# A four-layer mixer stack: decay sums broadcast by DMA, S5 inputs loaded from another queue, S5 output matrices in a ring of three

## The chip, the cores and the metric

The kernel runs on one core of one Trainium2 chip. The metric is the device time of one execution in microseconds: the median of three runs was 2107.67 (2106.01 to 2112.61). A single further execution was recorded by the hardware profiler and took 2112.38. All times inside the kernel are from that execution.

## What is computed

A sequence of 256 tokens of width 2048 passes through four layers, each a different mixer, and after each one the result is added to the residual and normalised:

```python
h = x
for i in range(4):                     # ssd, fox, mla, s5
    out = mixer[i](h, ...)
    h = layer_norm(ALPHA * h + out, ln_g[i], ln_b[i])
```

Layer 0 (ssd) works on 8 groups of 8 heads. For a group it needs, in each of two chunks of 128 tokens, the running sums `acs` of the decay of each head, and from them a 128x128 matrix per head:

```python
seg = acs[..., :, None] - acs[..., None, :]
decay = exp(where(l >= s, seg, -inf))
y_diag = einsum('bcgls,bcgels,bcsgep->bclgep', cb, decay, xdt)
...
yg = yg * rsqrt(mean(square(yg), -1) + RMS_EPS)     # per group, ahead of the output matrix
```

Layer 1 (fox) is attention with a forget gate over 16 heads. Layer 2 (mla) is attention with low-rank projections. Layer 3 (s5) is a diagonal state-space layer: an input map, a scan over time of complex states, and an output map, then a gated linear unit. Everything is 32-bit.

## The kernel before

**Projections.** Every large matrix product is done in three passes. `half` (L89) loads half of a weight block, 512 KB, into one of 7 `raw` buffers through the SyncE queue (SP). ScalarE (ACT) rounds it to `whi` (L100), VectorE (DVE) forms the remainder `wlo` (L101); there are 4 buffers of each. TensorE (PE) then multiplies hi by hi, hi by lo and lo by hi (`mm3`, L107 to L109). One half is 24 matmuls of 256 columns (`proj_T`) or 12 of 512 columns (`proj_tok`).

**Order.** The program is written as one stream of projections. After each half `C.tick()` (L56) advances a counter and runs what `C.defer(n, fn)` (L51) had put off by n ticks. That is how side work (decays, scores, scans, transposes) gets its place between the halves. A scheduler then fixes the order on each engine; every engine and every DMA queue works strictly in its own order, so a waiting instruction holds all behind it. That goes for SP too: its queue carries the weight loads of all layers in one line.

**Layer 0, `ssd` (L424).** `group(g)` (L513) makes z (8 halves into `pt`), then B, C and four x strips (12 halves into `cps`), each with a short convolution. `decay(g)` (L501) works on `arena[:, 0:2048]`, called `seg`: four small GpSimd (POOL) DMAs bring the sums of two heads each to one partition of `rows`, four `partition_broadcast` instructions (L506) spread them over 128 partitions, 16 DVE instructions (L510) subtract and mask, ACT takes one exponential of 2048 columns (L511). `scores` multiplies by the score matrix (L535). `within` (L565) uses `seg` as weights of the matmuls `yd`. `gate` (L560) multiplies by z on POOL (L562) and squares on ACT (L563), `across` (L582) adds the state part on POOL (L587), takes an inverse square root in small DVE steps (`rsqrt`, L192) and scales on ACT (L593). `turn_y` (L598), 4 ticks later, transposes the result on PE (`ypt`, L605). Of group g, `within`, `across` and `turn_y` run while group g+1 is at its z and B halves.

**Layer 1, `fox` (L623)** carries the parameters of layer 3 along: `s5_params` (L905) is a generator, stepped once per head, whose 16 steps on POOL make the input, output and kernel matrices of S5 (`wn`, `pn`, `kt`) and store them to DRAM (`W_d`, `P_d`, `K_d`). Each step needs a tile `bc` of 128 KB of inputs, of which there are 4 buffers, loaded by SP (`load_bc`, L1048). PE transposes and multiplies what a step made (`wp`, L1028, and `kp`, L1035) one step later.

**Layer 3, `s5` (L1112).** Four input strips (`u_strip`), then 16 `z_tile`s of two halves each; between them the strips are turned, mapped into states (`enter`, matmuls `vp`), scanned on DVE (`scan`, L1149, three pieces of 1, 2 and 1 strips, about 1.9 us of it per tick), and mapped out in 8 halves (`y_half`, L1299: matmuls `near` with a tile `shifts` from `K_d`, then `far` with a tile `mats` from `P_d`). The tiles `mats` and `shifts` share one ring of 2 buffers, loaded by POOL's DMA queue (L1137, L1146). `y_load` of a half asks for its `mats`, then its `shifts`, and is called when the half before has been written into the program.

Of the kernel before, what the change touches and what calls it, by code (L numbers as in the profile page):

```python
# [19 lines left out]
P = 128  # L20
T = 256
# [402 lines left out]
def ssd(C, hT, out):  # L424
    nc, A = C.nc, C.A
    mm, tr = nc.tensor.matmul, nc.tensor.transpose
    G, E, NH = 8, 8, 64
    with C.tc.tile_pool(name="ssd", bufs=1) as sp, C.tc.tile_pool(name="ssd_c", bufs=1) as vp, C.tc.tile_pool(name="ssd_t", bufs=1) as tp:
# [69 lines left out]

        seg = arena[:, 0:2048].rearrange("p (e c l) -> p e c l", e=E, c=2)

        def decay(g):  # L501
            rows = tp.tile([P, 512], F32, tag="rows", name="rows", bufs=1)
            for r in range(4):
                nc.gpsimd.dma_start(rows[32 * r:32 * r + 1], acsT[g * E + 2 * r:g * E + 2 * r + 2, :])
            for r in range(4):
                nc.gpsimd.partition_broadcast(arena[:, r * 512:(r + 1) * 512], rows[32 * r:32 * r + 1])  # L506
            for c in range(2):
                for e in range(E):
                    s = acs_t[c][:, g * E + e:g * E + e + 1]
                    nc.vector.scalar_tensor_tensor(seg[:, e, c], seg[:, e, c], s, upm, op0=ALU.subtract, op1=ALU.min)  # L510
            nc.scalar.activation(arena[:, 0:2048], arena[:, 0:2048], AF.Exp)  # L511

        def group(g):  # L513
            zs = arena[:, 2048 + (g % 2) * 1024:2048 + (g % 2 + 1) * 1024].rearrange("p (t f) -> p t f", t=2)
# [11 lines left out]
            def scores():  # L526
                cbp = C.aux("cbp")
                for c in range(2):
                    cs = slice(c * P, (c + 1) * P)
                    mm(cbp[:, cs], bT[:, cs], cT[:, cs], start=True, stop=True)  # L530
                tr(cbp[:, 256:384], bT[:, 0:P], C.ident)
                S["btok"] = vp.tile([P, P], F32, tag="btok", name="btok")
                nc.scalar.copy(S["btok"], cbp[:, 256:384])
                m8 = arena[:, 0:2048].rearrange("p (e x) -> p e x", e=E)
                nc.vector.tensor_tensor(m8, m8, cbp[:, None, 0:256].to_broadcast([P, E, 256]), op=ALU.mult)  # L535

            C.defer(2, scores)
            xp = []

            def turn_x(k, xc):  # L540
# [41 lines left out]
            def across():  # L582
                xs, off, sq = S["xs"], S["off"], S["sq"]
                ops = C.aux("ops")
                mm(ops, cT[:, P:], S["st"], start=True, stop=True)
                nc.vector.tensor_tensor(heads(off), heads(ops), bc(eacs, g), op=ALU.mult)
                nc.gpsimd.tensor_tensor(xs[1], xs[1], off, op=ALU.add)  # L587
                gate(1)
                ms = tp.tile([P, 2], F32, tag="ms", name="ms")
                nc.vector.tensor_scalar(ms, sq, 1.0 / 512, 4 * RMS_EPS, op0=ALU.mult, op1=ALU.add)  # L590
                rs = C.rsqrt(ms, 2, "gr")
                for c in range(2):
                    nc.scalar.activation(xs[c], xs[c], AF.Copy, scale=rs[:, c:c + 1])  # L593
                C.defer(4, turn_y)
                if g == G - 1:
                    C.load_res(A["x"])

# [18 lines left out]
        for g in range(G):  # L616
            group(g)
        return C.out_layer(0, lambda cb, **kw: C.proj_tok([A["ssd_o"][cb, q] for q in range(8)], yT, **kw),
                           [(tp, t, 1, 1) for t in ("xs0", "xs1", "xdt0", "xdt1", "xdd", "st", "rows", "gb")],
                           [[(C.hp, f"h{n}{c}", 1) for n in "hl"] for c in range(4)], out)  # L620


# [282 lines left out]
def s5_params(C, sp, sq):  # L905
# [142 lines left out]
    def load_bc(n):  # L1048
        if n < 16:
            bcs[n] = sq.tile([P, 4, 4, 16], F32, tag="bc", name="bc", bufs=4)  # L1050
            nc.sync.dma_start(bcs[n], A["s5_bc"][n])

    turns = None
    for n in range(2):
# [57 lines left out]
def s5(C, hT, out):  # L1112
# [8 lines left out]
    with C.tc.tile_pool(name="s5", bufs=1) as sp, C.tc.tile_pool(name="s5_w", bufs=1) as wp, C.tc.tile_pool(name="s5_t", bufs=1) as tp:  # L1121
# [11 lines left out]
        uX, U = {}, {}  # L1133

        def mats(src):
            t = wp.tile([P, 1024], F32, tag="mats", name="mats", bufs=2)
            nc.gpsimd.dma_start(t, src)  # L1137
            return t

        def shifts(ft, h2):  # L1140

            t = wp.tile([P, 848], F32, tag="mats", name="shifts", bufs=2)
            for e in range(2):
                src = C.K_d[ft, h2, e].rearrange("i g b f -> i (g b f)")
                src = bass.AP(src.tensor, src.offset, [[16, L], list(src.ap[0]), [1, 848]])
                nc.gpsimd.dma_start(t[64 * e:64 * e + 64], src)  # L1146
            return t

        def scan(pc):  # L1149
# [6 lines left out]
            def mac(dst, src, n, w):  # L1156
                ar, ai = (a4[:, n, i, :, f0:f0 + nf].rearrange("p c f j -> p c (f j)") for i in range(2))
                if w:
                    ar, ai = (z[:, :, :, None].to_broadcast([P, 2, fj, w]) for z in (ar, ai))
                t = wp.tile([P, 2, 1024], F32, tag="sc", name="sc", bufs=1)  # L1160
                size = 2 * fj * (w or 1)
                t0, t1 = ((t[:, i, 0:size].rearrange("p (c j m) -> p c j m", c=2, m=w) if w else
                           t[:, i, 0:size].rearrange("p (c j) -> p c j", c=2)) for i in range(2))
# [7 lines left out]
                v.tensor_tensor(dst, dst, t0, op=ALU.add)  # L1171
                yield us

            at = lambda k, n=16: x[:, :, :, 16 * (k + 1):16 * (k + 1) + n]
            yield from mac(at(1), at(0), 0, 16)
            yield from mac(at(2), at(1), 0, 16)
            yield from mac(x[:, :, :, 1:16], at(2, 15), 0, 15)
            for m in range(1, 15):
                yield from mac(x[:, :, :, m + 1], x[:, :, :, m], 3, 0)
            for k in range(3):  # L1180
                yield from mac(at(k), x[:, :, :, 0:16], k, 16)

        def u_strip(ft):
            x = uX[ft] = sp.tile([P, L, 4, NC], F32, tag=f"ux{ft}", name=f"ux{ft}")
# [52 lines left out]
        def enter(ft, h2, un, w):  # L1237
# [52 lines left out]
        yh, yl = [None] * KB, [None] * KB  # L1290
        ys, ready = {}, []

        def y_load(ft, h2):
            pm = mats(C.P_d[ft].rearrange("p h c j f -> p h (c j f)")[:, 2 * h2:2 * h2 + 2]).rearrange(
                "p (g c q e f) -> p g c q e f", g=2, c=2, q=2, e=2)
            tm = shifts(ft, h2)
            C.defer(2, lambda: y_half(ft, h2, pm, tm))

        def y_half(ft, h2, pm, tm):  # L1299

# [25 lines left out]
            if h2 == 0:  # L1326
                y_load(ft, 1)
            else:
                C.defer(1, lambda: back1(ft, ys[ft]))

        def back1(ft, ys):
# [163 lines left out]
```

## Time and profile before

| what | us |
|---|---|
| median of three runs | 2107.67 |
| the profiled execution | 2112.38 |
| its span, first to last instruction | 2110.6 |
| PE busy | 2023.2 |
| DVE busy | 1380.9 |
| ACT busy | 955.6 |
| POOL busy | 424.8 |

The stages in the span: layer 0 from 0 to about 760 (its output projection from about 590), layer 1 to about 1290, layer 2 to about 1680, layer 3 to the end. A row of the profile's groups gives an engine, the source line, the tiles written and read, a count, the busy time and the mean duration. In a row of the view of waits stand the engine and line that waited, what released it, the time in total, how often, and the longest. In a row of the view by stretches stand the start and the end, the length, the busy time of PE, of its weight load, of DVE, ACT and POOL, each with its instructions, then the granted clock, the share of the DMA engines and GB/s.

### The profile page before, as it was taken

The numbers are of one execution on the slowest core, as the hardware profiler recorded it, in microseconds if no ns is written. First come the engines' busy times: TensorE is split into PE (matmuls) and PEld (weight loads), VectorE is DVE, ScalarE is ACT, GpSimd is POOL, SyncE is SP. The second block draws the span as 40 slices with busy tenths as digits, with TensorE's granted clock in tenths as the row PEclk, the third lists the DMA queues.
The fourth block names the chain that finished last, engine by engine and source line by source line (L and its number), as shares of the span: only waits on it lengthen the run. The fifth ranks groups of instructions, "written<-read, shape, count | busy, mean of one in ns | idle before, by whom it ended". The sixth has DMA issues, their size and how long they took to land.

```text
span 2110.6 us, 36624 instructions
## 1 busy us (share of the span) xinstructions
PE 2023.2 (96%) x14409; PEld 1834.6 (87%) x14409; DVE 1380.9 (65%) x2393; ACT 955.6 (45%) x1434; POOL 424.8 (20%) x522
## 2 busy tenths in 40 slices
PE   8999999999999999899999999999999998988997
PEld 7889888898878877799999978998888798988986
DVE  6776777677654695465555567646556787975656
ACT  5454555455443333344444444544554354444442
POOL 0211222122200027988870000000000001010002
PEclk9999999999999999899999999999999999999999
DMA  8445444544475545465666564664347555675662
GB/s 281 158 141 171 150 160 161 163 150 155 159 233 189 186 147 177 175 216 172 225 194 202 177 208 128 202 184 143 111 144 239 183 174 177 193 225 166 187 189 100
DMA packets 117292, 374.32 MB, mean 177 GB/s; under 512 B 18992, under 2 KB 23552, under 8 KB 116352
## 3 DMA queue, kind: packets, MB, share of 16 engines
q1 hardware_dynamic: 105440, 350.20, 51.9%
q0 software_dynamic: 6912, 16.14, 2.5%
q10 hardware_dynamic: 4768, 5.64, 0.8%
q8 instruction: 113, 1.85, 0.4%
q14 instruction: 59, 0.48, 0.1%
HBM read 357.81 MB, written 14.04 MB: 176 GB/s over the span
## 4 chain that ended last, share of the span: by engine, by line
PE 80%; DVE 8%; POOL 4%; DMA 4%; issue 2%; ACT 1%; SPq 0%; DVEq 0%; POOLq 0%; ACTq 0%
PE pt L109 10%; PE pt L107 10%; PE pt L108 10%; PE cps L108 4%; PE cps L107 4%; PE cps L109 4%; PE zps L107 4%; PE zps L109 4%; PE zps L108 4%; DMA shifts<-K_d 2%; DVE wlo L101 2%; PE pk L185 2%; PE pk L187 2%; PE pk L186 2%; PE gps L107 1%
## 5 line engine op out<-in xcount | busy, mean ns | idle before, releaser
L101 DVE TENSOR_TENSOR wlo<-raw,whi 128x1024 fp32r<-128x1024 f32 (+3 forms) x611 | 758.1, 1243 | 469.1 <-ACT whi L100 457.1
L100 ACT CAST whi<-raw 128x1024 fp32r<-128x1024 f32 (+3 forms) x611 | 632.0, 1036 | 803.3 <-PE pt L109 294.6
L107 PE MATMUL pt<-whi,hh 128*128 128x512 f32 (+2 forms) x716 | 281.7, 394 | 11.4 <-ACT whi L100 11.0
L109 PE MATMUL pt<-whi,hl 128*128 128x512 f32 (+2 forms) x716 | 279.8, 391 | 0.6 <-DVE hl L330 0.4
L108 PE MATMUL pt<-wlo,hh 128*128 128x512 f32 (+2 forms) x716 | 278.4, 389 | 1.6 <-DVE wlo L101 1.5
L107 PE MATMUL zps<-hh,whi 128*128 128x256 f32 x768 | 221.1, 288 | 1.0 <-ACT whi L100 1.0
L109 PE MATMUL zps<-hh,wlo 128*128 128x256 f32 x768 | 218.5, 285 | 1.3 <-DVE wlo L101 1.3
L108 PE MATMUL zps<-hl,whi 128*128 128x256 f32 x768 | 218.4, 284 | 0.0
L108 PE MATMUL cps<-hl,whi 128*128 128x256 f32 x768 | 217.6, 283 | 0.0
L109 PE MATMUL cps<-hh,wlo 128*128 128x256 f32 x768 | 217.6, 283 | 0.0
L107 PE MATMUL cps<-hh,whi 128*128 128x256 f32 x768 | 217.6, 283 | 0.0
L107 PEld LDWEIGHTS pt<-whi,hh 128*128 128x128 f32 x716 | 136.2, 190 | 39.2 <-ACT whi L100 11.4
L108 PEld LDWEIGHTS pt<-wlo,hh 128*128 128x128 f32 x716 | 136.2, 190 | 29.9 <-DVE wlo L101 3.9
L109 PEld LDWEIGHTS pt<-whi,hl 128*128 128x128 f32 x716 | 136.4, 190 | 27.4 <-issue 1.7
L107 PEld LDWEIGHTS zps<-hh,whi 128*128 128x128 f32 x768 | 148.3, 193 | 1.6 <-ACT whi L100 1.2
L109 PEld LDWEIGHTS zps<-hh,wlo 128*128 128x128 f32 x768 | 148.3, 193 | 1.5 <-DVE wlo L101 1.5
L108 PEld LDWEIGHTS zps<-hl,whi 128*128 128x128 f32 x768 | 148.3, 193 | 0.0
L108 PEld LDWEIGHTS cps<-hl,whi 128*128 128x128 f32 x768 | 147.5, 192 | 0.3
L107 PEld LDWEIGHTS cps<-hh,whi 128*128 128x128 f32 x768 | 147.4, 192 | 0.3
L109 PEld LDWEIGHTS cps<-hh,wlo 128*128 128x128 f32 x768 | 147.4, 192 | 0.1
L107 PE MATMUL pt<-whi,yh 128*128 128x512 f32 x240 | 95.8, 399 | 0.0
L108 PE MATMUL pt<-wlo,yh 128*128 128x512 f32 x240 | 95.5, 398 | 0.0
(505 smaller groups left out, 4295.5 us busy)
## 6 DMA issues: line engine op xcount, KB each, us to landing
raw<-in_ssd_z SPq DMA_DIRECT2D x64, 512.0 KB
raw<-in_ssd_x SPq DMA_DIRECT2D x64, 512.0 KB
raw<-in_ssd_o SPq DMA_DIRECT2D x64, 512.0 KB
raw<-in_fox_v SPq DMA_DIRECT2D x32, 512.0 KB
raw<-in_fox_q SPq DMA_DIRECT2D x32, 512.0 KB
raw<-in_fox_k SPq DMA_DIRECT2D x32, 512.0 KB
raw<-in_fox_z SPq DMA_DIRECT2D x32, 512.0 KB
raw<-in_fox_o SPq DMA_DIRECT2D x32, 512.0 KB
```

Of the source, the lines that this page charges most:

```text
L100: nc.scalar.copy(hi, r)
L101: nc.vector.tensor_tensor(lo, r, hi, op=ALU.subtract)
L107: mm(ps, s[0], m[0], start=first, stop=False)
L108: mm(ps, s[0], m[1], start=False, stop=False)
L109: mm(ps, s[1], m[0], start=False, stop=last)
L185: mm(o, ws[0], a[0], start=kb == 0 and c % 2 == 0, stop=False)
L186: mm(o, ws[0], a[1], start=False, stop=False)
L187: mm(o, ws[1], a[0], start=False, stop=end)
```

## The change

Three places.

Layer 0: the running sums go to a DRAM tile `acs_d` once, and `decay_load(g)` fills `arena[:, 0:2048]` by one DMA from POOL's queue that reads the 8 KB of a group 128 times. `rows` and the four `partition_broadcast` are gone. The DVE part of `decay` comes 2 ticks after the load (1 tick for group 0), goes head by head, and ACT takes the exponential in four parts of 512 columns; the product with the scores is two instructions of 1024. `scores` is put off by 3 ticks, not 2, and `turn_y` by 6, not 4. Two tiles `gb0`, `gb1` stand in for `rows` and `gb` in the list of buffers that the normalisation may use.

Layer 1: `load_bc` issues from POOL's queue.

Layer 3: the ring has 3 buffers; `y_load(k)` asks for `shifts` first, then `mats`; it is called as the half before is about to be written, and `outputs` writes a half when its piece is scanned and 3 ticks have passed since its load. The first load stands behind the last strip's `enter`, not behind the first scan. To make room, the scan's work tile is halved, so that the piece of two strips is scanned in runs of 8 columns of time, not 16.

```diff
@@ ssd
+        acs_d = C.dp.tile([NH, T], F32, name="acs_d")
...
+            nc.scalar.dma_start(acs_d, acsT)
...
-            decay(0)
+            decay_load(0)
+            C.defer(1, lambda: decay(0))
...
+        def decay_load(g):
+            src = acs_d[g * E:(g + 1) * E, :].rearrange("e l -> (e l)")[None, :]
+            nc.gpsimd.dma_start(arena[:, 0:2048], src.to_broadcast([P, 2048]))
+
         def decay(g):
-            rows = tp.tile([P, 512], F32, tag="rows", name="rows", bufs=1)
-            for r in range(4):
-                nc.gpsimd.dma_start(rows[32 * r:32 * r + 1], acsT[g * E + 2 * r:g * E + 2 * r + 2, :])
-            for r in range(4):
-                nc.gpsimd.partition_broadcast(arena[:, r * 512:(r + 1) * 512], rows[32 * r:32 * r + 1])
-            for c in range(2):
-                for e in range(E):
+            for e in range(E):
+                for c in range(2):
...
-            nc.scalar.activation(arena[:, 0:2048], arena[:, 0:2048], AF.Exp)
+                if e % 2:
+                    x = arena[:, (e - 1) * T:(e + 1) * T]
+                    nc.scalar.activation(x, x, AF.Exp)
...
-                decay(g)
+                decay_load(g)
+                C.defer(2, lambda: decay(g))
...
-            C.defer(2, scores)
+            C.defer(3, scores)
...
-                C.defer(4, turn_y)
+                C.defer(6, turn_y)
@@ s5_params
-            nc.sync.dma_start(bcs[n], A["s5_bc"][n])
+            G.dma_start(bcs[n], A["s5_bc"][n])
@@ s5
-            t = wp.tile([P, 1024], F32, tag="mats", name="mats", bufs=2)
+            t = wp.tile([P, 1024], F32, tag="mats", name="mats", bufs=3)
...
-                t = wp.tile([P, 2, 1024], F32, tag="sc", name="sc", bufs=1)
+                t = wp.tile([P, 2, 512], F32, tag="sc", name="sc", bufs=1)
...
-            yield from mac(at(1), at(0), 0, 16)
-            yield from mac(at(2), at(1), 0, 16)
-            yield from mac(x[:, :, :, 1:16], at(2, 15), 0, 15)
+            wide = 16 // nf
+            spans = [(m, wide) for m in range(0, 16, wide)]
+            for k in range(2):
+                for m, n in spans:
+                    yield from mac(at(k + 1, m, n), at(k, m, n), 0, n)
...
+                if pc == 2:
+                    y_load(0)
+                    C.defer(1, outputs)
...
-                for i, ft in enumerate(range(FIRST[pc], FIRST[pc] + SIZE[pc])):
-                    C.defer(1 + 4 * i, lambda ft=ft: y_load(ft, 0))
...
+        def y_load(k):
+            ft, h2 = divmod(k, 2)
+            tm = shifts(ft, h2)
             pm = mats(...)
-            tm = shifts(ft, h2)
-            C.defer(2, lambda: y_half(ft, h2, pm, tm))
+            held.append((k, C.now, tm, pm))
+
+        def outputs():
+            k, since, tm, pm = held[0]
+            if PIECE[k // 2] in done and C.now >= since + 3:
+                held.pop()
+                if k < 7:
+                    y_load(k + 1)
+                y_half(k // 2, k % 2, pm, tm)
+            if held:
+                C.defer(1, outputs)
```

How the instructions stand: POOL in layer 0, before, from the first group's broadcast for the second group to its end. `xs` are the two chunks of the group's output, `arena` the broadcast target or z.

```order
L506 ISA
L506 ISA arena<-rows 128x512
L562 ISA
L562 TENSOR_TENSOR xs_968<-xs_968,arena 128x512
L506 ISA
L506 ISA arena<-rows 128x512
L587 ISA
L587 TENSOR_TENSOR xs_969<-xs_969,off 128x512
L506 ISA
L506 ISA arena<-rows 128x512
L562 ISA
L562 TENSOR_TENSOR xs_969<-xs_969,arena 128x512
```

The same engine and place in the changed kernel.

```order
L561 TENSOR_TENSOR xdd<-xdt_968,tok 128x512
L506 DMA arena<-acs_d 128x2048
L568 TENSOR_TENSOR xs_966<-xs_966,arena 128x512
L593 TENSOR_TENSOR xs_967<-xs_967,off 128x512
L568 TENSOR_TENSOR xs_967<-xs_967,arena 128x512
```

The broadcasts and the bare ISA rows between the gates are gone, and one DMA stands ahead of the gates. On PE, the 8 transposes `ypt` of a group stood behind the next group's 288 matmuls of `cps` and some of the z after it; now they stand behind the first 48 of `cps`. From the end of `yd` to `ypt` there are now the two of `sps`, 59 of `pt`, the two of `ops` and 48 of `cps`. On DVE the 16 subtractions now stand right behind the product `off` of the group before, ahead of and between the steps of its inverse square root, with the rounding remainders `wlo` in between.

SP in layer 1, before: the weight loads of `fox` with the inputs `bc` of S5 among them.

```order
L676 DMA ck<-cum_d 128x256
L95 DMA raw<-in_fox_v 128x1024
L1051 DMA bc<-in_s_bc 128x256
L95 DMA raw<-in_fox_v 128x1024 x3
L1051 DMA bc<-in_s_bc 128x256
L95 DMA raw<-in_fox_v 128x1024 x3
L95 DMA raw<-in_fox_q 128x1024 x2
L95 DMA raw<-in_fox_k 128x1024
L1051 DMA bc<-in_s_bc 128x256
L95 DMA raw<-in_fox_k 128x1024
```

The same place in the changed kernel.

```order
L682 DMA ck<-cum_d 128x256
L95 DMA raw<-in_fox_v 128x1024 x7
L95 DMA raw<-in_fox_q 128x1024 x2
L95 DMA raw<-in_fox_k 128x1024 x2
L95 DMA raw<-in_fox_z 128x1024 x2
L95 DMA raw<-in_fox_q 128x1024 x2
```

The loads of `bc` have left SP; on POOL four of them now stand ahead of the first step, and one behind the arithmetic of each of the first twelve steps, ahead of the store of `P_d`. PE's order in this layer is the same.

POOL's DMAs in layer 3, before: `mats<-W_d` are input matrices, the others belong to the output halves.

```order
L1137 DMA mats<-W_d 128x1024 x4
L1137 DMA mats<-P_d 128x1024
L1146 DMA shifts<-K_d 64x1x848 x2
L1137 DMA mats<-P_d 128x1024
L1146 DMA shifts<-K_d 64x1x848 x2
L1137 DMA mats<-W_d 128x1024 x2
L1137 DMA mats<-P_d 128x1024
```

The same in the changed kernel.

```order
L1143 DMA mats<-W_d 128x1024 x5
L1152 DMA shifts<-K_d 64x1x848 x2
L1143 DMA mats<-P_d 128x1024
L1152 DMA shifts<-K_d 64x1x848 x2
L1143 DMA mats<-P_d 128x1024
L1152 DMA shifts<-K_d 64x1x848 x2
L1143 DMA mats<-P_d 128x1024
```

All input matrices are now loaded ahead of the first output half, and in a ring of three the `shifts` of a half take the buffer of the `mats` two halves earlier. On PE the 8 halves stand more evenly: 72 matmuls of `zps` or more between two of them, but only 24 ahead of the last one.

More of the change, by code (lines that the diff above doesn't have):

```diff
@@ L533, in scores @@
                 nc.scalar.copy(S["btok"], cbp[:, 256:384])
-                m8 = arena[:, 0:2048].rearrange("p (e x) -> p e x", e=E)
-                nc.vector.tensor_tensor(m8, m8, cbp[:, None, 0:256].to_broadcast([P, E, 256]), op=ALU.mult)
-            C.defer(2, scores)
+                for e in range(0, E, 4):
+                    m4 = arena[:, e * T:(e + 4) * T].rearrange("p (e x) -> p e x", e=4)
+                    nc.vector.tensor_tensor(m4, m4, cbp[:, None, 0:256].to_broadcast([P, 4, 256]), op=ALU.mult)
+            C.defer(3, scores)
             xp = []
@@ L618, in ssd @@
         return C.out_layer(0, lambda cb, **kw: C.proj_tok([A["ssd_o"][cb, q] for q in range(8)], yT, **kw),
-                           [(tp, t, 1, 1) for t in ("xs0", "xs1", "xdt0", "xdt1", "xdd", "st", "rows", "gb")],
+                           [(tp, t, 1, 1) for t in ("xs0", "xs1", "xdt0", "xdt1", "xdd", "st", "gb0", "gb1")],
                            [[(C.hp, f"h{n}{c}", 1) for n in "hl"] for c in range(4)], out)
@@ L1140, in shifts @@
         def shifts(ft, h2):
-            t = wp.tile([P, 848], F32, tag="mats", name="shifts", bufs=2)
+            t = wp.tile([P, 848], F32, tag="mats", name="shifts", bufs=3)
             for e in range(2):
@@ L1172, in mac @@
                 yield us
-            at = lambda k, n=16: x[:, :, :, 16 * (k + 1):16 * (k + 1) + n]
-            yield from mac(at(1), at(0), 0, 16)
-            yield from mac(at(2), at(1), 0, 16)
-            yield from mac(x[:, :, :, 1:16], at(2, 15), 0, 15)
+            at = lambda k, m, n: x[:, :, :, 16 * (k + 1) + m:16 * (k + 1) + m + n]
+            wide = 16 // nf
[3 more added lines that the diff above has]
+                    yield from mac(at(k + 1, m, n), at(k, m, n), 0, n)
+            for m, n in spans:
+                n = min(n, 15 - m)
+                yield from mac(x[:, :, :, 1 + m:1 + m + n], at(2, m, n), 0, n)
             for m in range(1, 15):
@@ L1180, in scan @@
             for k in range(3):
-                yield from mac(at(k), x[:, :, :, 0:16], k, 16)
+                for m, n in spans:
+                    yield from mac(at(k, m, n), x[:, :, :, m:m + n], k, n)
         def u_strip(ft):
@@ L1291, in s5 @@
         ys, ready = {}, []
-        def y_load(ft, h2):
+        held = []
+        def y_load(k):
+            ft, h2 = divmod(k, 2)
+            tm = shifts(ft, h2)
             pm = mats(C.P_d[ft].rearrange("p h c j f -> p h (c j f)")[:, 2 * h2:2 * h2 + 2]).rearrange(
                 "p (g c q e f) -> p g c q e f", g=2, c=2, q=2, e=2)
-            tm = shifts(ft, h2)
-            C.defer(2, lambda: y_half(ft, h2, pm, tm))
+            held.append((k, C.now, tm, pm))
[8 more added lines that the diff above has]
+                C.defer(1, outputs)
         def y_half(ft, h2, pm, tm):
@@ L1325, in y_half @@
                 nc.vector.tensor_tensor(y[:, b::2], y[:, b::2], far[b][:, 0:4 * NC].rearrange("p (g c) -> p g c", g=4), op=ALU.add)
-            if h2 == 0:
-                y_load(ft, 1)
-            else:
+            if h2:
                 C.defer(1, lambda: back1(ft, ys[ft]))
```

## The prediction

> **What bounds the kernel now.** The page comes first, its busy times.
>
> ```profile
> span 2110.6 us, 36624 instructions
> PE 2023.2 (96%) x14409; PEld 1834.6 (87%) x14409; DVE 1380.9 (65%) x2393; ACT 955.6 (45%) x1434; POOL 424.8 (20%) x522
> ```
>
> PE is at work 96% of the span, so the time is PE's work plus PE's gaps, 2110.6 - 2023.2 = 87.4 us, plus whatever its work is stretched by a lower clock. The change takes no large matmul away. It can only win gaps and clock. The next view, the waits of PE, says where the gaps are.
>
> ```profile
> PE near L1311 <- DMA shifts<-K_d: 23.2, 7, 6.8
> PE ypt L605 <- ACT xs L593: 19.5, 7, 4.8
> PE pt L107 <- ACT whi L100: 11.0, 2, 7.3
> ```
>
> These three rows are 53.7 of the 87.4 us, and each of the three edits aims at one of them: the loads of layer 3 (`shifts`), the output turn of layer 0 (`ypt`) and one place in layer 1 (the two waits for `whi` lie there). The third view cuts the span at those places: for layer 0 the seven groups from one `yd` to the next, with one good group alone, then three pieces of layer 1 and two of layer 3, with 40 us of the scan alone.
>
> ```profile
> core 0: us, PE busy (x) PEld busy (x) DVE busy (x) ACT busy (x) POOL busy (x), PEclk, DMA share, GB/s
> 85.40:570.10 484.70, 466.16 (x3117) 424.89 (x3117) 349.55 (x583) 244.05 (x346) 97.87 (x95) 0.98 0.49 157
> 226.80:292.20 65.40, 65.34 (x447) 59.58 (x447) 50.66 (x84) 34.85 (x50) 12.58 (x14) 1.00 0.51 169
> 854.40:873.06 18.66, 16.39 (x120) 15.98 (x121) 6.53 (x6) 6.16 (x8) 17.16 (x28) 0.91 0.90 320
> 873.06:903.28 30.22, 22.78 (x179) 22.14 (x178) 13.19 (x20) 9.13 (x16) 28.01 (x39) 0.83 0.32 108
> 903.28:923.61 20.33, 20.33 (x179) 20.02 (x178) 13.62 (x19) 9.15 (x16) 18.97 (x27) 1.00 0.69 233
> 1752.60:1898.70 146.10, 129.22 (x1601) 126.58 (x1599) 122.36 (x246) 62.57 (x103) 12.54 (x21) 0.95 0.66 194
> 1800.00:1840.00 40.00, 40.00 (x413) 39.80 (x412) 39.62 (x52) 16.11 (x21) 1.81 (x3) 1.00 0.58 172
> 1898.70:1918.90 20.20, 13.38 (x246) 12.74 (x245) 4.36 (x8) 4.62 (x7) 1.81 (x3) 0.75 0.45 144
> ```
>
> A gap costs twice: the wait itself, and a granted clock of 0.75 to 0.98 in the pieces that hold waits, against 1.00 in those without. So each place is priced by its length against the length that it has without a wait.
>
> **Layer 0: 20 us.** With no wait the seven groups would take 7 x 65.4 = 457.8 us, so 484.7 - 457.8 = 26.9 us are to be had. The wait is made on POOL:
>
> ```profile
> POOL arena L506 <- issue: 155.2, 25, 7.0
> ```
>
> Before 25 of the broadcasts POOL stands for about 6.2 us (155.2 / 25) with nothing to wait for. A group has four, and its gate and its state part stand behind them in POOL's order, so `xs` comes late and `ypt` meets it. The change takes the four broadcasts away, and `ypt` comes 2 ticks later. What it adds is one transfer of 1 MB into `seg`, issued when `yd` has read the old one. DVE's 16 subtractions wait for it; behind them on DVE are the small steps of `rsqrt` and the `wlo` of the next halves, behind the exponentials on ACT the scaling of `xs` and the next `whi`. So the question is whether the transfer lands before PE has used up its lead. The rows for that sum, first the durations, then the landings for `acsT` (2 KB each) and for `mats` (512 KB each):
>
> ```profile
> 67.87 4.69 DVE L510 SCALAR_TENSOR_TENSOR arena<-arena,tok,upm 128x128 f32<-128x128 f32 x16
> 140.84 1.22 DVE L101 TENSOR_TENSOR wlo<-raw,whi 128x1024 fp32r<-128x1024 f32 x1
> 141.98 0.15 DVE L203 SCALAR_TENSOR_TENSOR ny<-nt,seed 128x2 f32<-128x2 f32 x1
> 142.16 0.16 DVE L201 SCALAR_TENSOR_TENSOR nt<-ny 128x2 f32<-128x2 f32 x1
> 143.34 1.33 ACT L593 ACTIVATE xs<-xs,ny 128x512 f32<-128x512 f32 x2 [2.15 <-DVE ny L203]
> 88.89 0.91 PE sps L572 x2
> 91.20 0.86 PE ops L585 x2
> 781.85 1.05 ACT L100 CAST whi<-raw 128x1024 fp32r<-128x1024 f32 x1 [1.66 <-PE pt L109]
> 784.57 1.06 ACT L100 CAST whi<-raw 128x1024 fp32r<-128x1024 f32 x1 [1.67 <-PE pt L109]
> 114.38 1.05 ACT L100 CAST whi<-raw 128x1024 fp32r<-128x1024 f32 x1 [1.83 <-PE cps L108]
> 117.26 1.05 ACT L100 CAST whi<-raw 128x1024 fp32r<-128x1024 f32 x1 [1.06 <-PE cps L108]
> ```
>
> ```profile
> DMA to landing us min/median/max: 1.5/2.3/3.8
> ```
>
> ```profile
> L1137 POOL DMA_DIRECT2D mats<-P_d x8: 528/580/582, 1747.7 to 1900.2; - x8
> ...
> DMA to landing us min/median/max: 4.0/6.1/8.5
> ```
>
> PE's lead from `yd` to `ypt` in the new order is `sps` 0.91, five halves into `pt` at 2.72 (784.57 - 781.85), `ops` 0.86, and two halves into `cps` at 2.88 (117.26 - 114.38): 0.91 + 13.6 + 0.86 + 5.76 = 21.1 us. Besides the landing it must hold the issue 0.58, the subtractions 4.69, some 12 small steps at 0.18 (2.2), two `wlo` 2.4 and the scaling 1.33: 11.2 us. A landing of up to 21.1 - 11.2 = 9.9 us is hidden. No row has a transfer of 1 MB. I estimate it as two of 512 KB less one of 2 KB, since a fixed part is counted once: 2 x 4.0 - 1.5 = 6.5 at the least, 9.9 at the median, 13.2 at the most. Weighted one, two, one, with 0, 0 and 3.3 us too late, that is 0.8 us a group; I take 1.0, because a write into 128 partitions from one 8 KB row may be worse than a plain load. 26.9 - 7 x 1.0 = 20. Bounds: 27, if all land early, and 2, if all take 13.2 (7 x 3.3 = 23, a little clock with it). DVE has room: 349.55 of 484.70 us.
>
> The nearest row has half a MB landing in 4.0 to 8.5 us. The Trainium skill, page "DMA: Bandwidth & Descriptors", section "Measured (HBM→SBUF, 128 partitions, SWDGE, issued from GpSimd)", gives 6.15 us of busy DMA engines for 1 MB; by that the landing would be hidden, and this term 27, not 20. No run here shows 1 MB yet.
>
> **Layer 1: 9 us.** SP's queue, its waits first, then one step on each engine:
>
> ```profile
> SPq L1051 <- POOL t L1093: 139.1, 11, 16.3
> ```
>
> ```profile
> 884.64 0.33 SPq L1051 DMA_DIRECT2D bc<-in_s_bc  x1
> 820.43 0.89 PE L1035 MATMUL kp<-pn,bd 128*32 128x64 f32 x16
> 853.58 0.78 PE L1035 MATMUL kp<-pn,bd 128*32 128x64 f32 x14 [0.83 <-POOL pn L1097]
> 853.83 0.93 POOL L1103 DMA_DIRECT2D P_d<-pn  x1 [0.30 <-POOL pn L1097]
> 902.30 0.93 POOL L1103 DMA_DIRECT2D P_d<-pn  x1 [0.30 <-POOL pn L1097]
> 891.72 1.22 PE L417 MATMUL o<-pt,V 128*128 128x256 f32 x2 [7.44 <-ACT pt L411]
> ```
>
> SP stands up to 16.3 us at a `bc` load until POOL has used the buffer, and all weight loads stand behind it; at 884.64 the load goes out, and behind it the weights and inputs that PE lacks until 891.72, a wait of 7.44. Issued by POOL, the load waits for POOL's own work only, and SP goes on. The piece 873.06 to 903.28 then takes the 20.33 us of the next head, which has the same 179 matmuls: 30.22 - 20.33 = 9.9. What is late next is POOL: PE would reach the third `kp` at about 820.4 + 0.9 + 8 x 2.72 + 2.2 (two `wp`, one `kp`) = 845, and `pn` is there at 853.5, by two issues of 0.58 later. So PE waits some 10 us there, where it now waits 0.83 because its weights were late as well. What is won ahead of that is lost there again; the 9.9 behind it stays, less about 0.9 for the issues: 9. After it POOL keeps up: it made three steps in 902.30 - 853.83 = 48.5 us, 16.2 each, and with an issue 16.7, where a head of PE takes 20.33. Bounds: 4, if the low clock after a wait of 10 us (0.83 after that of 7.44) costs 5 us more, and 9.9 + 3.7 = 13.6, if the other wait for `whi` (11.0 - 7.3 = 3.7) goes too, with POOL's step there shorter.
>
> **Layer 3: 21 us.** With a ring of two, `shifts` of a half stands in POOL's queue behind `mats`, which waits for `far` of the half before; that is 23.2 us in seven waits. In the ring of three `shifts` goes out a whole half earlier. Six of the seven waits lie in the stretch 1752.60 to 1898.70: PE's work there is 129.22 us at a clock of 0.95, 122.8 at full clock, so at most 146.10 - 122.8 = 23.3 could go. But DVE is busy 122.36 us there, and the scan's runs of 8 add to it, by these two rows:
>
> ```profile
> 1802.85 1.22 DVE L1167 TENSOR_TENSOR sc<-X,a4s 128x1024 f32<-128x1024 f32 x1
> 1825.34 0.68 DVE L1167 TENSOR_TENSOR sc<-X,a4s 128x512 f32<-128x512 f32 x1
> ```
>
> Two halves cost 2 x 0.68 - 1.22 = 0.14 more; some 24 such splits are 3.4 us. DVE then needs 125.8, which allows 146.1 - 125.8 = 20.3. DVE is full in the middle already (39.62 of 40), but not at the ends, so I take 15, with 8 and 23 as bounds. In the last stretch the wait of 6.8 goes, and with it the clock of 0.75: 13.38 x 0.75 = 10.0 at full clock. New there is a wait for the last `mats`, which goes out after `near` of the seventh half. These rows of the chain show its cover:
>
> ```profile
> 1898.80 1.02 PE near L1311 x30
> 1899.88 1.02 PE far L1320 x62
> ```
>
> Cover is 1.02 + 2.88 + 1.02 = 4.9 us, needed 0.58 + 6.1, so 1.8 us of wait, and 2 more of lower clock: 20.2 - 13.8 = 6 (3 to 9). Together 21, from 11 to 32.
>
> The row of `mats` has POOL's issues at 0.53 to 0.58 us, in a stretch where DVE is busy 84% of the time. The Trainium skill speaks against the change on the same page, section "SWDGE vs HWDGE vs iDMA": descriptors for POOL's transfers are written by POOL itself into SBUF, and VectorE in its two-port mode locks it out. By that rule the broadcasts would come late wherever DVE is at work, which leads to the slower rival below; by the row, whose issues stay at 0.58, the sum stands.
>
> **Sum.** 20 + 9 + 21 = 50. The profiled execution took 2112.4: 2112.4 - 50 = 2062.4. The median of three runs lies 4.7 lower (2112.38 - 2107.67): 2057.7, or **2058**.
>
> **Rivals.**
> - DVE bounds layer 3: the stretch gains 2, not 15. For it: 39.62 of 40 us. Against: 122.36 of 146.10 over the whole. 2058 + 13 = 2071. Chance 0.16.
> - POOL bounds layer 1: from 854.40 to 903.28 it is busy 17.16 + 28.01 = 45.2 of 48.9 us; if it can't run faster than that, 3.7 are left, less two issues 2.5. Against: 16.2 us a step. 2058 + 6.5 = 2064. Chance 0.10.
> - The broadcast lands at 13.2 us in every group: layer 0 wins 2 to 3. 2058 + 17.5 = 2075. Chance 0.08.
> - The waits only move: SP, freed in layer 1, and PE meet the next late thing everywhere, and 2 to 3 us are left: 2105. Against: the rows without waits reach a clock of 1.00. Chance 0.04.
> - Slower: one row read 128 times is much slower than a plain load. At a landing of L each group waits L - 9.9, and this decides when 7 x (L - 9.9) passes 26.9 + 30, at L = 18. At 20 us: 70.7 - 56.9 = 14 over: 2122. For it: nothing like it is in the trace. Against: 13.2 is the worst that the rows give. Chance 0.04.
>
> **The numbers.** The forecast has 0.58. A difference under 0.3%, 6.3 us, is about what a measurement of this kernel can't tell from none. Faster by more: forecast and the first three rivals, 0.92; within: 0.04; slower: 0.04. The range: at the low end 27 of layer 0, 13.6 of layer 1 and 29 of layer 3, 2108 - 70 = 2038; at the high end the late broadcast and POOL's bound together, 2058 + 17.5 + 6.5 = 2082. Outside are the last two rivals and the far ends, under 2 in 10.
>
> **What would show it.** In the waits of PE: `ypt`, `near`, and `o` gone, and about 10 us at `kp` for `pn`. The seven layer-0 groups at 66 us each, the transfer into `seg` landing in under 10 us; the piece of layer 1 at 20.3 us; no SP wait at the `bc` load. In the scan DVE without gaps and PE with waits of a few us for `wlo`. The sum is wrong if the broadcasts land late (PE then waits for `whi` and `wlo` in layer 0), if POOL's steps are over 20.3 us, or if layer 3 stays at 140 us or more.

## The result

The changed kernel took 2053.76 us (median of 4 runs, 2052.46 to 2055.91) against 2110.14 for the kernel before: a ratio of 0.9732, 95% interval 0.9711 to 0.9754. Its profiled execution has a span of 2054.1, 56.5 less than before's. The busy times from its page, after the change:

```profile
span 2054.1 us, 36447 instructions
PE 2004.6 (98%) x14409; PEld 1821.1 (89%) x14409; DVE 1383.0 (67%) x2425; ACT 956.7 (47%) x1458; POOL 401.8 (20%) x482
```

PE has the same 14409 matmuls, yet its busy time fell by 18.6 us. Most of that is the clock: by the trace's record of it PE was at work for 48.2 us at half clock before and for 17.2 now, and half of the difference is 15.5. The other 37.9 are gaps, 87.4 before and 49.5 now. The waits of PE, its first rows and those of layer 1:

```profile
PE pt L107 <- ACT whi L100: 6.9, 1, 6.9
PE yp L1361 <- DVE ys L1352: 6.1, 2, 5.4
PE pt L108 <- DVE wlo L101: 4.4, 5, 1.9
...
PE far L1347 <- DMA mats<-P_d: 3.1, 1, 3.1
PE wp L1034 <- POOL wn L1101: 2.8, 1, 2.8
PE kp L1041 <- POOL pn L1103: 2.1, 1, 2.1
...
PE kp L1041 <- POOL pn L1096: 1.9, 1, 1.9
```

`near`, `ypt` and `o` have no row any more. What is left of the wait for `whi` is the one at the very start of the program. Before it was 7.3 there, and only the other, of 3.7, lay in layer 1: where the prediction says that both lie there, it misread the row. New are `yp` and `far` in layer 3, and POOL in layer 1.

The large weight matmuls are the same 11568 in both kernels and in nearly the same order, so the two traces can be laid side by side by their number. This is the start of some of them:

| number | place | before | after | difference |
|---|---|---|---|---|
| 432 | layer 0, second group begins | 75.1 | 73.6 | -1.6 |
| 816 | layer 0, third group begins | 137.3 | 141.3 | +4.0 |
| 3299 | layer 0, last `ypt` over | 602.8 | 574.2 | -28.6 |
| 4224 | layer 1, first `kp` over | 821.2 | 792.7 | -28.6 |
| 4584 | layer 1, behind the repaired place | 903.9 | 863.1 | -40.7 |
| 8849 | layer 2, in its output projection | 1621.1 | 1580.1 | -41.0 |
| 9149 | layer 3, in its input | 1692.0 | 1654.4 | -37.6 |
| 10392 | layer 3, behind the seventh half | 1900.7 | 1848.7 | -52.0 |
| 10429 | layer 3, behind the last half | 1919.1 | 1862.4 | -56.7 |

So layer 0 is worth 28.6, layer 1 12.1, layer 3 14.4 in the scan and 4.7 at its last half, and 3.4 are lost in layer 2's output projection. The stretches of the changed kernel that answer to those of before: the seven groups, one group alone, the piece of layer 1, the scan, and the last half.

```profile
88.68:534.87 446.19, 446.19 (x3076) 410.72 (x3076) 339.37 (x588) 241.37 (x364) 63.65 (x50) 1.00 0.56 182
278.29:342.36 64.07, 64.07 (x442) 58.97 (x442) 49.48 (x85) 34.62 (x53) 9.09 (x8) 1.00 0.57 181
842.17:862.54 20.37, 20.37 (x180) 20.06 (x178) 12.24 (x19) 9.16 (x16) 19.15 (x28) 1.00 0.66 210
1715.12:1848.73 133.61, 126.89 (x1696) 124.45 (x1695) 125.81 (x270) 64.38 (x105) 13.65 (x23) 0.97 0.70 203
1848.73:1862.36 13.63, 10.51 (x156) 10.12 (x151) 4.02 (x9) 3.13 (x6) 0.03 (x1) 0.87 0.68 261
```

In the seven groups PE is busy every microsecond at full clock, 64.1 us a group. (The stretch holds 41 matmuls fewer than before's, since `yd` now stands at the same place of every group; that is why its gain of 38.5 is not the layer's.) In the scan DVE is busy 125.81 of 133.61 us. How the broadcast does, first its issue on POOL, then its landing:

```profile
L506 POOL DMA_DIRECT2D arena<-acs_d x8: 591/591/727, 58.8 to 474.6; - x8
...
DMA to landing us min/median/max: 5.0/6.7/8.5
```

### The profile page after: what moved, and what is told of

Read it like the earlier page. It is cut to its first block, busy times and chain, and to the rows that moved or that the text cites. A ratio compares the mean times of both kernels' runs of the same rounds, so it can differ in the third digit from the quotient of the medians.

```text
span 2054.1 us, 36447 instructions
## 1 busy us (share of the span) xinstructions
PE 2004.6 (98%) x14409; PEld 1821.1 (89%) x14409; DVE 1383.0 (67%) x2425; ACT 956.7 (47%) x1458; POOL 401.8 (20%) x482
## 4 chain that ended last, share of the span: by engine, by line
PE 83%; DVE 9%; DMA 3%; POOL 2%; issue 2%; ACT 1%; SPq 0%; DVEq 0%; POOLq 0%; ACTq 0%
PE pt L108 10%; PE pt L109 10%; PE pt L107 10%; PE cps L109 4%; PE cps L108 4%; PE cps L107 4%; PE zps L107 4%; PE zps L108 4%; PE zps L109 4%; DVE wlo L101 2%; PE pk L185 2%; PE pk L186 2%; PE pk L187 2%; PE fox_q L107 2%; PE fox_q L108 2%
## 5 line engine op out<-in xcount | busy, mean ns | idle before, releaser
L109 PE MATMUL pt<-whi,hl 128*128 128x512 f32 (+2 forms) x716 | 275.6, 385 | 0.6 <-DVE hl L330 0.4
```

Source lines behind the costliest of these rows:

```text
L109: mm(ps, s[1], m[0], start=False, stop=last)
```

## The experiments

Times are medians; "slower" and "faster" by so many microseconds are against the changed kernel's 2053.76, and ratios against runs of the kernel before on the same chip. The kernel before is itself less steady than the changed one (2099.37 to 2108.42 over 7 runs in one place, 2107.16 to 2116.72 over 7 in another), so a ratio can be off by a few tenths of a per cent from the difference of medians. The runs come from several chips, and by the ratios the differences below are `turn4` +29, `bcast2` +12, `ring2` +13, `step` -7, `back2` -6, `narrow` +6 and `step_back` -13 us: the signs stand, the sizes to some 5 us.

**Each part alone.** `l0_only` is the kernel before with the hunks of `ssd`, `l1_only` with that of `s5_params`, `l3_only` with those of `s5`:

```diff
@@ l1_only
-            nc.sync.dma_start(bcs[n], A["s5_bc"][n])
+            G.dma_start(bcs[n], A["s5_bc"][n])
```

> The kernel before with the part of layer 0 alone. My theory: the three parts act apart, and this one is worth what its stage shows between the two traces, 28.6 us (ratio 0.986 to 0.987). Rival: what layer 0 wins is given back later (another stage sets the pace), then under 15 us. The waits of TensorE for xs at ypt are gone.

> The kernel before with the loads of bc on POOL's queue alone. My theory: 12 us (ratio 0.994), a wait of some 7 us at wp and kp for POOL in place of those for whi and o. Rival: POOL's own steps grow by more than the issues and it is worth 2 to 4 us.

> The kernel before with the part of layer 3 alone. My theory: 15 to 20 us (ratio 0.991 to 0.993): the near waits of 23.2 go, some 3 us come back at the last mats and 5 to 6 at ys because DVE is full in the scan. Rival: the scan in shorter runs costs what the ring wins, under 8 us.

Measured: 2082.79 (ratio 0.9889, 0.9867 to 0.9910), 2099.25 (0.9953, 0.9935 to 0.9971) and 2089.04 (0.9920, 0.9895 to 0.9946), where the kernel before took 2109.74. That is 27.0, 10.5 and 20.7 us, 58.2 together, and all three at once gave 56.4. By the ratios the parts are worth 23, 10 and 17 us, 50 together; each of them is known to about 5 us, so the parts add up as far as these runs can tell. The waits of PE in each, in the same order:

```profile
PE near L1317 <- DMA shifts<-K_d: 21.5, 9, 5.5
PE o L417 <- ACT pt L411: 8.3, 1, 8.3
```

```profile
PE near L1311 <- DMA shifts<-K_d: 22.6, 8, 6.0
PE ypt L605 <- ACT xs L593: 19.5, 8, 3.9
```

```profile
PE ypt L605 <- ACT xs L593: 18.0, 8, 3.8
...
PE o L417 <- ACT pt L411: 9.2, 1, 9.2
PE yp L1355 <- DVE ys L1346: 6.0, 2, 5.4
...
PE far L1341 <- DMA mats<-P_d: 3.0, 1, 3.0
```

Each part takes away its own waits and leaves the others about as they were. What comes new lies in the same layer (`yp` and `far` in `l3_only`, 6.1 us at `wp` and `kp` in `l1_only`), but for some 2 us more at `kp` in `l0_only`. The rivals of all three expectations fell. No run takes the hunk of `ssd` apart any further than the turn below, so what the order of the subtractions and the exponential in four parts give by themselves stays open.

**Only the later turn.**

```diff
@@ turn6_only (the kernel before)
-                C.defer(4, turn_y)
+                C.defer(6, turn_y)
```

> The kernel before with turn_y put off by 6 ticks, not 4, and nothing else; the four broadcasts stay. Theory A (POOL's broadcasts are the cause, but PE only met them at ypt, 4.8 us at the longest, and two halves are 5.4): the waits at ypt go and 15 to 25 us of the 28.6 are won by the later turn alone. Theory B (POOL's late gate also holds other things, the broadcast by DMA is what counts): under 8 us, the wait moves to the next thing that hangs on xs or on seg.

Measured: 2116.36, ratio 1.0029 (1.0010 to 1.0049): nothing won, rather a little lost. Its waits of PE and of POOL in layer 0:

```profile
PE ypt L605 <- ACT xs L593: 19.1, 9, 3.5
```

```profile
POOL arena L506 <- issue: 119.8, 20, 6.6
```

The wait at `ypt` is what it was. Counted in the traces, the first `ypt` of the first seven groups stands 350 to 360 weight matmuls behind `yd` in the kernel before, and here 346 to 357; in the changed kernel it is 95 in the first group and 107 in the next six. This looks as if the scheduler puts `ypt` where it reckons `xs` to be ready, which with the broadcasts on POOL is nearly a whole group later, whatever the tick says; the reckoning itself stands in no row. Theory B holds in its first half (the broadcast by DMA is what counts); where it expected the wait to move on, the wait did not move at all.

**The earlier turn, with the DMA broadcast.**

```diff
@@ turn4 (the changed kernel)
-                C.defer(6, turn_y)
+                C.defer(4, turn_y)
```

> The changed kernel with turn_y put off by 4 ticks again, not 6. Theory of the forecast's lead sum: the lead from yd to ypt shrinks by two halves into cps (5.8 us) to some 15.3, what it must hold is 11.2 and a landing of 6.7, 17.9: 2 to 3 us of wait at ypt in each of 8 groups, with the lower clock 20 to 30 us slower than the changed kernel (2075 to 2085). Rival: the sum counts steps that overlap, xs is ready much earlier, and it is within 4 us of the changed kernel (2050 to 2058).

Measured: 2078.53, 24.8 slower (ratio 0.9871, 0.9847 to 0.9895). The first row of its waits of PE, and the stretch of one group:

```profile
PE ypt L611 <- ACT xs L599: 14.5, 9, 2.3
```

```profile
352.60:420.70 68.10, 65.94 (x442) 60.26 (x442) 48.79 (x85) 34.85 (x53) 9.04 (x8) 0.97 0.52 170
```

A wait of 1.6 us in the mean, 2.3 at the longest, and a group is 4.0 us longer (68.1 against 64.1), the lower clock included. With the broadcast in place the tick does set the place of `ypt` (59 weight matmuls behind `yd`, not 107), and the lead of 15.3 us is 1.6 to 2.3 short, so 16.9 to 17.6 must be held; the sum said 17.9 with a landing of 6.7, and 18.7 with this run's own median of 7.5. So the lead sum is shown at its edge, 1 to 2 us too cautious, and the 2 ticks are a needed part of the change, though worth nothing alone.

**The broadcast twice.**

```diff
@@ bcast2 (the changed kernel)
-            nc.gpsimd.dma_start(arena[:, 0:2048], src.to_broadcast([P, 2048]))
+            [nc.gpsimd.dma_start(arena[:, 0:2048], src.to_broadcast([P, 2048])) for _ in range(2)]
```

> The changed kernel with the broadcast of a group issued twice into the same place (2 MB). Theory of the lead sum: it lands some 4 to 6 us later, at 11 to 13, over the 9.9 that are hidden: 1 to 3 us a group, 8 to 25 us slower than the changed kernel. Rival: there is more slack than the sum says, under 5 us slower.

Measured: 2061.62, 7.9 slower (0.9788, 0.9773 to 0.9804). Where the time lies decides, not its size. By the numbered matmuls it is 8.0 behind the changed kernel at number 816, and 8.1 at number 3300: all of it is lost around the first group's decay, nothing in the other seven. So the size is the theory's but the place is not, and for seven groups the rival (more slack) came true. POOL waits for the first transfer before it issues the second:

```profile
POOL arena L506 <- DMA arena<-acs_d: 44.5, 8, 6.7
```

So the second landed some 13 us (2 x 6.7) after the first was issued, and in seven groups it was hidden. This doesn't refute the lead sum, since the order on DVE is another one: from the second group on eight of the 16 subtractions stand ahead of the small steps of the inverse square root in the changed kernel, and none here. It does show that the first group has no slack: there the landing is on PE's path.

**The ring of two in the new order.**

```diff
@@ ring2 (the changed kernel)
-            t = wp.tile([P, 1024], F32, tag="mats", name="mats", bufs=3)
+            t = wp.tile([P, 1024], F32, tag="mats", name="mats", bufs=2)
...
-            t = wp.tile([P, 848], F32, tag="mats", name="shifts", bufs=3)
+            t = wp.tile([P, 848], F32, tag="mats", name="shifts", bufs=2)
...
-                if k < 7:
-                    y_load(k + 1)
                 y_half(k // 2, k % 2, pm, tm)
+                if k < 7:
+                    y_load(k + 1)
```

> The changed kernel with the ring of two again and the loads of the next half asked for behind the half, shifts first; the halves stand at the same places on TensorE as in the changed kernel. Theory of the forecast (the third buffer lets shifts go out a half earlier): the waits at near come back, 10 us or more. Rival (the order shifts before mats and the wider spacing, three ticks between the load and its half, hide the loads without a third buffer): within 4 us of the changed kernel but for the last halves, where no tiles lie between.

Measured: 2061.50, 7.7 slower (0.9792, 0.9775 to 0.9809). The first row of its waits of PE:

```profile
PE near L1338 <- DMA shifts<-K_d: 8.3, 2, 7.0
```

By the numbered matmuls it is level with the changed kernel through the scan (2.3 ahead at number 9500, 1.5 ahead at 10400) and 7.7 us worse at the last half, where 7.0 of the wait lies. The rival holds: in the scan a ring of two serves as well. What took the six other waits away is the order (`shifts` ahead of `mats`) and the place of the halves: `near` of two halves of a strip stand 72 weight matmuls apart, not 44 to 48 as before. Which of the two counts for more no run tells. The third buffer pays at the last half alone.

**One step of the parameters less ahead of the heads.**

```diff
@@ step (the changed kernel)
             v_strip(cb)
-            next(steps)
+            if cb < 3:
+                next(steps)
```

> The changed kernel without the step of the parameters behind the last value strip of layer 1, so that the third wp and kp come a head later and no two steps meet on TensorE. Theory: the 6.9 us that TensorE waits at wp and kp for POOL go with their low clock, 6 to 9 us faster (2045 to 2048), since POOL's 16 to 17 us a step fit into a head of 20.3. Rival: POOL is the bound there, and the wait comes back at the next kp: within 3 us.

Measured: 2043.08, 10.7 faster (0.9700, 0.9686 to 0.9715). PE's rows of `wp` and `kp` around the place, first in the changed kernel:

```profile
815.55 0.89 PE L1041 MATMUL kp<-pn,bd 128*32 128x64 f32 x16
816.37 0.33 PE L1034 MATMUL wp<-ident,wn 128*128 128x128 f32 x1
819.54 0.55 PE L1034 MATMUL wp<-ident,wn 128*128 128x128 f32 x3 [2.85 <-POOL wn L1101]
822.03 0.42 PE L1041 MATMUL kp<-pn,bd 128*32 128x64 f32 x2 [1.94 <-POOL pn L1096]
824.51 1.28 PE L1041 MATMUL kp<-pn,bd 128*32 128x64 f32 x14 [2.07 <-POOL pn L1103]
```

then in this one:

```profile
813.44 0.89 PE L1042 MATMUL kp<-pn,bd 128*32 128x64 f32 x16
832.28 0.60 PE L1035 MATMUL wp<-ident,wn 128*128 128x128 f32 x4
832.81 0.89 PE L1042 MATMUL kp<-pn,bd 128*32 128x64 f32 x16
```

Two steps met on PE, and the second was not ready; a head apart, no step waits. POOL was late only there: behind it the steps follow PE's heads. More was won than the waits of 6.9, because the low clock went too: in the changed kernel the granted clock is 0.50 from 820.0 to 830.3, which stretches the work behind the waits (5.8 us of it from 824.5) to twice its length.

**The place of `yp`, the width of the scan, and both repairs together.**

```diff
@@ back2 (the changed kernel)
-                C.defer(1, lambda: back1(ft, ys[ft]))
+                C.defer(3, lambda: back1(ft, ys[ft]))
@@ narrow (the changed kernel)
-            wide = 16 // nf
+            wide = 8 // nf
```

`step_back` has the edits of `step` and `back2`.

> The changed kernel with the turning back of an output strip in layer 3 (yp) two ticks later. Theory A (DVE is full in the scan and ys is late, but the place of yp decides whether TensorE meets it): the wait of 5.4 at yp goes with its low clock, 4 to 8 us faster than the changed kernel (2046 to 2050). Theory B (DVE is the bound of that stretch): the time is the same within 2 us, the wait turns up at the next wlo.

> The changed kernel with the scan in runs half as wide again (4 columns of time for two strips, 8 for one), about a hundred instructions more on DVE. If DVE is the bound of layer 3, 98 more instructions at some 0.14 us each, 10 to 14 us, show in full. Rival: DVE has gaps enough at the ends of the scan, and under 4 us show.

> Both edits that take a wait away: the step of the parameters behind the last value strip left out, and yp two ticks later. If the two act apart: 10 to 11 us for the first and what the second gives alone, 2036 to 2039 if that is 4 to 7. Rival: the second is worth nothing, 2043.

Measured: `back2` 2049.14, 4.6 faster (0.9704, 0.9684 to 0.9725); `narrow` 2060.09, 6.3 slower (0.9762, 0.9739 to 0.9784); `step_back` 2041.19, 12.6 faster (0.9670, 0.9648 to 0.9693). In `narrow` the scan has 360 instructions and 118.1 us on DVE, in the changed kernel 264 and 102.8, so 15.2 us more of DVE's work cost 6.3, between the two expectations. But PE doesn't lose it in the scan: `narrow` is 4.7 ahead of the changed kernel at number 9500 and 9.1 ahead at 10392, with one half less done, and only at 10429 is it 1.6 behind. The longer scan pushes the halves back, so that the last two stand together at the end, with waits of 3.3 at `yp` and 4.5 at `far`. So what more DVE work costs shows at the end of the scan, not in it. In `back2` the 5.4 at `yp` went, but PE now waits once for `yt`, which hangs on the same DVE:

```profile
PE far L1347 <- DVE yt L1377: 3.3, 1, 3.3
```

By the numbered matmuls `back2` gains nothing in the scan (2.8 ahead at number 9500, 2.5 at 10400) and 4.5 at the last half. So in the scan theory B holds, the wait only moves; the gain comes from the end, where theory A had not looked: the wait of 3.1 at `far` is gone there, because the last `mats` landed in 4.2 us, not in 7.8. Why it landed sooner is not shown. `step_back` is the fastest of all, and the second repair is worth only 1.9 on top of the first, in medians whose ranges lie apart (2042.79 to 2043.88, 2039.22 to 2042.04): less than the 4.6 that it gave alone. But `step` and `step_back` ran on different chips, and by the ratios `step` is worth 6.7, `back2` 5.9 and both 13.1: whether the two add up stays open.

## Why the prediction was right

The total was forecast as 2058 and came out at 2053.8, faster and in the range. The mechanisms that it named hold in layers 0 and 1; in layer 3 the size came out, but the third buffer, named as the cause, did only the smaller part. Point by point:

- **Layer 0, forecast 20, found 28.6** in the profile (27.0 alone). The mechanism holds: POOL's stands before the broadcasts are gone, `ypt` waits for nothing. The term was mis-sized at the landing. The step "two of 512 KB less one of 2 KB" gave 6.5, 9.9 and 13.2 us; measured were 5.0, 6.7 and 8.5, all under the 9.9 that the lead hides. The residual of 1.0 us a group was therefore nil, and the term its upper bound of 27; the traces' 28.6 lies a little above it, as a group takes 64.1 us and not the 65.4 of the group it was priced by (442 matmuls, there 447). The sum also counts the issue of 0.58 twice, since the landing runs from the start of the issue: the transfer issued at 218.21 let DVE go on at 226.05, 7.84 later, within the landings of 5.0 to 8.5. The Trainium skill's 6.15 us for 1 MB (page "DMA: Bandwidth & Descriptors", section "Measured (HBM→SBUF, 128 partitions, SWDGE, issued from GpSimd)") would have given that bound: the trace's median is 6.7 with the source read 128 times. The rule that was weighed against the change (the Trainium skill, the same page, section "SWDGE vs HWDGE vs iDMA": VectorE can lock POOL out of the place where it writes its descriptors) did not show: the eight issues took 0.591 to 0.727 us. Whether VectorE was ever in the mode that locks, no trace tells.
- **What it said of `ypt`'s place was wrong.** "`ypt` comes 2 ticks later" is true of the call, but on PE it came some 250 weight matmuls earlier (107 instead of 350 to 360 behind `yd`). The lead of 21.1 was summed over the new order, which is why the sum held; `turn4` measured its edge at 16.9 to 17.6 against 17.9. The first group was not priced: the new way through DRAM costs it waits of 1.6 and 1.0 us on PE in this execution, 0.3 and 0.6 in all in those of `step` and `narrow`. (The table shows 5.5 from number 432 to 816; the other 2.9 are the eight `ypt` and 13 small matmuls of the next group, which now lie ahead of number 816.)
- **Layer 1, forecast 9, found 12.1** (10.5 alone), within 4 to 13.6. The waits of 1.0 and 1.3 at `zps` and their low clock, in the piece ahead of 873.06, went too, which the sum had not counted. SP's stands at `bc` are gone; the piece takes 20.37 us, forecast 20.33. PE's wait at the third `kp` came as foretold: PE stood from 816.7 to 824.5, 7.8 us with 6.9 of it as waits, forecast some 10, and the low clock behind it, which the sum put only into its lower bound, was there too. POOL kept up after it.
- **Layer 3, forecast 21, found 19.1.** 15 for the scan became 14.4; the splits cost DVE 3.9 us (240 to 264 instructions, whose durations add to 98.95 and 102.84), forecast 3.4, and PE was left with 5.4 at `yp`. 6 for the end became 4.7: the last `mats` came 3.1 us late, forecast 1.8, since it took 7.8 us to land and the sum had taken the median of 6.1. But the reason given, that "in the ring of three `shifts` goes out a whole half earlier", is not what took the waits of the scan away; `ring2` shows that order and spacing did, and that the third buffer is worth its 7.7 us at the end alone.
- **Not foreseen: 3.4 us lost ahead of layer 3**, between numbers 8849 and 9149, at a wait for `wlo` of 1.9. It is no part of the change: `ring2` and `step`, with the same instructions there, did not lose it (they come out of it 2.8 and 2.6 ahead of the changed kernel), while `l1_only`, without layers 0 and 3 changed, lost most of it. It varies from execution to execution; what made `wlo` late is not shown.

The errors of the terms, +8.6, +3.1, -1.9 and -3.4, add to 6.4 and stand against the forecast of 50: 56.4.

## What to carry to other kernels

A thing that is late on a side engine does not only cost the wait that the trace shows; as it seems from `turn6_only` and `turn4`, a scheduler that knows of it moves what hangs on it far back, and a hand-set delay then does nothing until the cause is gone. To know what a change of several edits was worth, number the instructions that both kernels share and compare their starts: that gives the gain place by place, while a list of waits leaves out the clock. After a repair, look for where two late things meet: the 7 us that PE now waited for POOL were ended by taking one step a head later, without any change of the work.

## What the runs showed of the hardware

- POOL stood for 6 to 8 us at most changes between `partition_broadcast` and its ordinary instructions, in both directions: by the view of waits 155.2 us in 25 cases ahead of the broadcasts, 49.7 in 7 ahead of L562 and 38.8 in 5 ahead of L587, with nothing to wait for. Two rows of the kernel before, a multiplication that follows a broadcast and the broadcast behind it, and then two rows of the view by source line:

```profile
136.82 1.28 POOL L562 TENSOR_TENSOR xs<-xs,arena 128x512 f32<-128x512 f32 x1 [7.24 <-issue]
143.97 1.17 POOL L506 PARTITION_BROADCAST arena<-rows  x1 [5.88 <-issue]
```

```profile
L506 POOLq MODIFY_POOL_CONFIG  x58: 1/5/37, 57.9 to 553.8; - x58
L562 POOLq MODIFY_POOL_CONFIG  x28: 129/129/129, 95.0 to 544.9; - x28
```

The instructions of the last two rows are the bare ISA rows in the order of POOL: they come in pairs, one pair ahead of each such change, 116 in layer 0 before and none there in the changed kernel. So the stand goes with what these instructions do, by their name a change of POOL's configuration. The Trainium skill (page "GPSIMD Engine Reference", section "2.1 Instruction dispatch") knows of about 6 us when a kernel that was just loaded is called for the first time; that fits the size, but here it came again and again. That code is loaded anew each time is an inference, not shown by a row. In the changed kernel, without these broadcasts, POOL has no such stand in layer 0.
- A wait of 1.9 us can bring the clock down, and need not: behind the wait for `wlo` the matmuls of 512 columns start 0.43 us apart and not 0.23, from 1595.0 to 1598.4. Rows of the changed kernel:

```profile
1594.14 0.50 PE L108 MATMUL pt<-wlo,hh 128*128 128x512 f32 x1 [1.86 <-DVE wlo L101]
...
1595.42 0.63 PE L109 MATMUL pt<-whi,hl 128*128 128x512 f32 x1
1595.85 0.63 PE L107 MATMUL pt<-w_zs,hh 128*128 128x512 f32 x1
...
1598.36 0.39 PE L107 MATMUL pt<-w_zs,hh 128*128 128x512 f32 x1
1598.59 0.40 PE L108 MATMUL pt<-w_zs,hh 128*128 128x512 f32 x1
```

In `narrow` the same matmul waited just as long, and the spacing stayed 0.23:

```profile
1590.93 0.50 PE L108 MATMUL pt<-wlo,hh 128*128 128x512 f32 x1 [1.86 <-DVE wlo L101]
1591.27 0.39 PE L109 MATMUL pt<-whi,hl 128*128 128x512 f32 x1
1591.50 0.40 PE L107 MATMUL pt<-whi,hh 128*128 128x512 f32 x1
```

In `turn4`, of seven waits at `ypt`, those of 1.2 and 2.0 us left the clock alone and the other five, of 2.0 to 2.3, were each followed by 3.41 us at half clock. In the traces' record of the clock every such stretch before the program's end is a whole multiple of 3.41 us, and within one execution all begin on one grid of that step. It is likely that the place of a wait on this grid decides, but no run tests it. So a wait can cost about twice its length, and the same wait in the next execution nothing but itself.
